# A diffusion trunk step on one core: first weights, conditioning pieces and column sums of the start reordered

## The chip, the core and the metric

The kernel runs on one core of one Trainium2 chip. The metric is the device time of one execution, in microseconds (us). Before the change it is 2101.41 us, the median of three runs (2099.74, 2101.41 and 2103.39).

## What is computed

One inference step of a two-layer trunk over 640 positions (128 of context, 512 latent) of 2048 features. Each layer modulates a normed input, multiplies it by a wide input matrix, mixes, gates, and multiplies by an output matrix:

```
def modulation(cond, w, b):
    m = jax.nn.silu(cond) @ w + b
    return jnp.split(m, 3, axis=-1)

shift, scale, gate = modulation(c, ada_w[l], ada_b[l])
h = rms_norm(x, norm_g[l]) * (1.0 + scale) + shift
y, side = even_mixer(h, w_in_even[e], ...)     # odd layers: odd_mixer
x = x + gate * (y @ w_out[l])
```

There are two condition vectors: one for the context, one for the latent positions. Only the shift and the scale of the first layer concern the change: 2 x 2048 columns of a matrix with 2048 rows, 33.55 MB in float32.

## The kernel before

The features of the input lie on partitions: 16 feature tiles (KT) of 128, each with 640 positions. A weight chunk is 128 output columns by 2048 rows. Every float32 product with weights is made of three passes in a reduced format (`mm_k`, L877): the high part of the weights with the high part of the input, high with low, low with high. For one feature tile k, one chunk and one half of the positions (320 or 322 columns with the two shift columns) these are three matmuls; this text calls each of them a wide matmul. ScalarE (ACT) makes the high part of a weight unit of four feature tiles (512 columns, 262 KB), GpSimd (POOL) its low part (`wpump`, L768). Units of the first chunks go to tiles `suhi`, `sulo`, the others to `whi`, `wlo`.

The start (`start`, L1544) does two things at once. For each of the 16 feature tiles f it brings the modulation matrix's columns of that tile as four **pieces** of 524 KB (`load`, tensor `ada0`) into a ring of NR = 7 buffers, and multiplies each piece by the condition vectors (`tiles`, L1588): four matmuls with 32 stationary columns, one for each 32-column strip of TensorE, so that the result of a tile is four partial sums that lie at partitions 0, 32, 64 and 96 of one bank. ACT copies the bank to SBUF, and two matmuls with a selection matrix `sel` add the four partial sums and bring them to columns (L1604, L1605): this text calls the pair a **column sum**. With it VectorE (DVE) makes scale and shift of the tile, and ACT and DVE the high and low part of the modulated input (`act_mod`, tiles `acth`, `actl`). A piece's buffer is loaded anew when its matmuls have run; the tile of x (`load_x`, 3 buffers) when its modulated input is made.

As soon as inputs are ready, wide matmuls of the first eight chunks run between the pieces: chunks 0 and 1 for every feature tile (`lead`), chunks 2 to 7 in windows of 2, 2, 4 and 4 feature tiles. That makes 2 x 16 x 6 + 6 x 12 x 6 = 624 wide matmuls in the start. What is left of chunks 2 to 7 follows after it, then all the rest of the program, where TensorE takes wide matmuls nearly without a break.

The order of the instructions on every engine is not written by hand. The kernel is built by a planner that keeps a clock for each engine and for the DMA (`Pace`, `pe` at L402, `dma` at L417) and lets tasks yield until their inputs would be ready by these clocks. A matmul's price and the rate of the DMA (330e3 bytes per us, L427) decide which instruction is written next, in the start and after it. The instructions of each engine then run in that order on the chip. All loads of the start are issued by SyncE (SP) in order, and each load also waits for the one eight places ahead of it in the sequence of all DMAs.

Of the kernel before, what the change touches and what calls it, by code (L numbers as in the profile page):

```python
# [14 lines left out]
ALU = mybir.AluOpType  # L15
AX = mybir.AxisListType
# [16 lines left out]
NR = 4  # L33
CW = 2 + HT
RING = 2560
WINDOWS = ((0, 2), (2, 2), (4, 4), (8, 4))
PIECE = 512

near = (*range(8, 12), *range(4))
ORDERS = (*near, *range(12, 16), *range(4, 8)), (*near, *range(4, 8), *range(12, 16))  # L40
LEAD, FIRST = 2, 8
# [172 lines left out]
class Core:  # L214
# [5 lines left out]


SMALL = [
    ("sel", 2),
    ("ada_bT", 96),
    ("norm_gT", 32),
    ("final_gT", 16),
# [8 lines left out]
class Trunk:  # L235
# [9 lines left out]
    def __init__(self, tc, d, es):  # L245
# [14 lines left out]
        nc = self.nc  # L260
# [20 lines left out]
        at, c = 0, {}  # L281
        for name, w in SMALL:
            c[name] = small[:, at : at + w]
            at += w
        self.sel = c["sel"]
        self.adab = c["ada_bT"].rearrange("p (a b) -> p a b", b=48)
        self.ng = c["norm_gT"].rearrange("p (a b) -> p a b", b=KT)
        self.fg = c["final_gT"]
# [113 lines left out]
    def pe(self, cost, out, *ins):  # L402
        pc = self.pace
        o, i = [pc.span(out)], [pc.span(x) for x in ins]
        if pc.late:
            pc.due(o + i)
        at = pc.ready("t", o, i)
        self.now = pc.t["t"] = max(self.now, at) + cost + 0.0025
        pc.note("t", o, i, self.now)

    cap, hold = 2.0, 99.0
    share, soon = 0.0, 99.0
    force = busy = often = False
# [3 lines left out]
    def dma(self, out, in_):  # L417

        pc = self.pace
        o, i = [pc.span(out)], [pc.span(in_)]  # L420
        if pc.late:
            pc.due(o + i)
        n = int(np.prod(out.shape)) * 4

        def emit():
            at = pc.t["q"] = max(pc.t["q"], self.now, pc.ready("q", o, i)) + 0.45
            pc.t["d"] = max(pc.t["d"], at + 1.2) + max(0.09, n / 330e3)  # L427
            pc.note("q", o, i, pc.t["d"] + 1.0)
            self.nc.sync.dma_start(out, in_)  # L429

        if pc.ready("q", o, i) <= self.now + 0.1:
            emit()
        else:
            pc.late.append((emit, o + i, lambda: pc.ready("q", o, i)))
# [333 lines left out]
    def wpump(self, force=False):  # L768

        nc, pc = self.nc, self.pace  # L770
# [22 lines left out]
        if job[0] == "add":  # L793
            o, a, b = job[1]()
# [6 lines left out]
        _, key, raw, n, M = job  # L801
        if not force and self.now < self.wfree_at:
            return False
        if isinstance(raw, int):
            m = self.chunks[key[0]][0].shape[2]
            at = 512 * raw
            raw = self.wraws[:, at : at + n * m]
            plain = True
        else:
            raw, m, plain = raw(), 128, False  # L810
        raw = raw.rearrange("p (a b) -> p a b", b=m)
        lead = plain and (key[0] < LEAD or key[:2] == (LEAD, 0))
        if lead:
            if not self.su_free:
                return False
        else:
            a = self.space(n * M)
# [725 lines left out]

    def start(self):  # L1544
        nc, d, tc, Y = self.nc, self.d, self.tc, self.Y
        self.part_b = self.P([128, FIRST, 2], "part_b")
        with tc.tile_pool(name="su", bufs=1) as su:
            self.open_su(su, 6)
# [4 lines left out]
            sq, rt = self.adas[:, 0:T], self.adas[:, T : T + HT]  # L1553
            rows = Ring([self.adas[:, 960 + 256 * i : 1216 + 256 * i] for i in range(3)])

            NX, NR = 3, 7
            xs = [Y[:, i, :] for i in range(NX)]
            room = Y[:, 3:10, :].rearrange("p a b -> p (a b)")
            more = self.t(su, [128, 3, 1024], "more")
            ring = [room[:, 1024 * i : 1024 * i + 1024] for i in range(4)] + [more[:, i, :] for i in range(3)]  # L1560
            ring = [x.rearrange("p (a b) -> p a b", b=256) for x in ring]

            def load(j):
                if j < 4 * KT:
                    self.dma(ring[j % NR], d["ada0"][j // 4, :, 4 * (j % 4) : 4 * (j % 4) + 4, :])

            def load_x(f):
                if f < KT:
                    self.dma(xs[f % NX], d["xT"][:, f, :])
                    self.flags.add(f"xs{f}")  # L1570
# [1 line left out]
            banks = [[self.pj(), self.pj()], [self.pj(), self.pj()]]  # L1572
            pm, pw = self.sm(), self.sm()
            pws = Ring([self.sm(), self.sm()])
            pcol = Ring([pw[:, 400 + 4 * i : 404 + 4 * i] for i in range(4)])

            def squares():
                for f in range(KT):
# [9 lines left out]
            def tiles():  # L1588
                for f in range(KT):
                    for q in range(4):  # L1590
                        w = ring[(4 * f + q) % NR]
                        yield from self.until(w)
                        for j in range(4):
                            o, c = pm[32 * j : 32 * j + 32, 0:256], cond[:, 4 * q + j, :]
                            self.pe(0.15, o, c, w[:, j, :])
                            nc.tensor.matmul(o, c, w[:, j, :], start=(q == 0), stop=(q == 3))
                        load(4 * f + q + NR)
                        if q % 2:
                            yield
                    r = rows.next()  # L1600
                    nc.scalar.activation(r, pm[:, 0:256], AF.Copy)
                    yield from self.until(r)
                    p = pcol.next()
                    self.mm(p[:, 0:2], r[:, 128:256], self.sel)  # L1604
                    self.mm(p[:, 2:4], r[:, 0:128], self.sel)  # L1605
                    nc.vector.tensor_scalar(
                        self.A[0][:, f, :], p[:, 0:2], self.b1[:, 0, f : f + 1], self.ng[:, 0, f : f + 1], ALU.add, ALU.mult
                    )
                    sh = self.s("sh", 2)
                    nc.vector.tensor_scalar(sh, p[:, 2:4], self.adab[:, 0, f : f + 1], None, ALU.add)  # L1610
                    yield from self.wait(f"sq{f}")
                    self.act_mod(0, f, xs[f % NX], 0, T)
                    nc.scalar.activation(self.ah[:, f, 0:2], sh, AF.Copy)
                    nc.vector.tensor_tensor(self.al[:, f, 0:2], sh, self.ah[:, f, 0:2].bitcast(F32), ALU.subtract)
                    load_x(f + NX)
                    self.flags.add(f"act{f}")
# [25 lines left out]
                    else:  # L1642
                        nc.vector.tensor_tensor(y, y, p, ALU.add)

            for j in range(4):
                load(j)
            load_x(0)
            for j in range(4, NR):
                load(j)
            load_x(1)  # L1650
            load_x(2)
            crow = self.t(su, [32, 128], "crow")
            self.sink = self.P([128, 8], "sink")
            nc.scalar.dma_start(self.sink, d["attn_sink"].partition_broadcast(128))
# [22 lines left out]
            for c in range(LEAD):  # L1677
                self.settle()
                self.chunks[c][4](*banks[c])
                self.drop(*banks[c])  # L1680
        self.actset = "s"

    def ysum(self, c):

# [1173 lines left out]
def _consts():  # L2858
    f = np.float32
    t = np.arange(NLAT)  # L2860
    pos = np.stack([t // 64, t % 64], -1).astype(f)
    inv = (f(10000.0) ** (-np.arange(32, dtype=f) / f(32))).astype(f)
    ang = pos[:, :, None] * inv
    cos, sin = np.cos(ang).astype(f), np.sin(ang).astype(f)
    c4 = np.concatenate([cos[:, 0], cos[:, 0], cos[:, 1], cos[:, 1]], 1).T
    s4 = np.concatenate([-sin[:, 0], sin[:, 0], -sin[:, 1], sin[:, 1]], 1).T
    i = np.arange(128)
    em = np.zeros((128, 512), f)
    em[:, 0:128] = np.where(i[None, :] >= i[:, None], 0, NEG)
    em[:, 384:512] = np.where(i[None, :] <= i[:, None], 0, NEG)  # L2870
    sel = np.zeros((128, 2), f)
    for j in range(4):
        sel[32 * j, 0] = sel[32 * j + 1, 1] = 1
    m1 = np.ones((128, 128), f) + np.eye(128, dtype=f)
    mu = (i[:, None] < i[None, :]).astype(f)
    return {"cos": c4, "sin": s4, "emask": em, "sel": sel, "gla_m1": m1, "gla_mu": mu}


def _na_grid():
# [115 lines left out]
```

## Time and profile before

| | |
|---|---|
| median of three runs | 2101.41 us |
| the profiled execution | 2099.8 us |
| its span, first to last instruction | 2098.0 us |
| granted TensorE clock, mean | 0.996 |
| TensorE (PE) busy | 2050.6 us, 98% |
| DVE, ACT, POOL busy | 72%, 46%, 52% |
| moved by DMA | 412.48 MB, mean 197 GB/s |
| moved by DMA in the first 150 us | 46.59 MB, mean 311 GB/s |

The profile shows one execution. The profiled execution's own time is 1.8 us above its span and 1.6 us below the median. TensorE is busy nearly throughout, but ends of matmuls are modelled, and a stretch that is full is not one at TensorE's peak: the spacing of the starts tells how fast it goes. Fractions of time in the start are read in stretches of the span, counted from its first instruction.

### The profile page before, as it was taken

What the parts mean: (1) busy time and instruction counts of PE and PEld (TensorE: products, weight loads), DVE (VectorE), ACT (ScalarE), POOL (GpSimd) and SP (SyncE); (2) the same over time, 40 slices, a digit from 0 to 9 for tenths busy, and PEclk for the clock granted to TensorE, in tenths of its full rate; (3) what the DMA queues carried; (4) which work ended last, traced back from release to release, by engine and by line L of the source; (5) the groups of instructions that cost most, each with busy time, mean ns of one, the idle gap of its engine ahead of it and who ended that gap; (6) DMA issues with size and microseconds to landing.
All of it is one profiled execution on the core that took longest, in us unless ns stands there. A gap on an engine that the chain in (4) does not pass through costs nothing. (4 is left out here: it accounts for less than half of the span.)

```text
span 2098.0 us, 39027 instructions
## 1 busy us (share of the span) xinstructions
PE 2050.6 (98%) x13990; PEld 1977.5 (94%) x13990; DVE 1500.2 (72%) x3448; ACT 962.7 (46%) x1997; POOL 1080.6 (52%) x817
## 2 busy tenths in 40 slices
PE   7999999999999999999999999999999999999996
PEld 4789999999999999999999999999999999999995
DVE  1337787787888786788777888887666677676565
ACT  3434453443334445444454544445454544454443
POOL 3433343333232223466556676656566567758883
PEclk9999999999999999999999999999999999999998
DMA  9955433335554443677657866756555575568756
GB/s 367 327 200 161 130 127 107 119 126 190 164 177 127 133 146 121 226 241 224 199 145 260 285 210 223 241 196 220 176 172 197 183 245 199 176 214 259 241 191 219
DMA packets 216306, 412.48 MB, mean 197 GB/s; under 512 B 25712, under 2 KB 89008, under 8 KB 216112
## 3 DMA queue, kind: packets, MB, share of 16 engines
q1 hardware_dynamic: 214640, 408.43, 59.0%
q8 instruction: 110, 1.80, 0.3%
q10 hardware_dynamic: 1472, 1.56, 0.2%
q14 instruction: 84, 0.69, 0.1%
HBM read 368.83 MB, written 38.45 MB: 194 GB/s over the span
## 5 line engine op out<-in xcount | busy, mean ns | idle before, releaser
L395 PE MATMUL bank<-acth,whi 128*128 128x320 f32 (+1 forms) x3144 | 963.6, 318 | 8.4 <-DVE arena L209 3.0
L395 PE MATMUL bank<-acth,wlo 128*128 128x320 f32 (+1 forms) x3144 | 938.3, 310 | 2.2 <-POOL wlo L209 2.2
L395 PE MATMUL bank<-actl,whi 128*128 128x320 f32 (+1 forms) x3144 | 937.7, 310 | 0.0
L209 POOL TENSOR_TENSOR wlo<-wraw,whi 128x512 fp32r<-128x512 f32 x364 | 507.1, 1399 | 705.7 <-ACT whi L209 609.1
L395 PEld LDWEIGHTS bank<-acth,whi 128*128 128x128 f32 x3144 | 583.1, 188 | 25.1 <-issue 8.8
L395 PEld LDWEIGHTS bank<-acth,wlo 128*128 128x128 f32 x3144 | 582.7, 188 | 3.0 <-POOL wlo L209 2.8
L395 PEld LDWEIGHTS bank<-actl,whi 128*128 128x128 f32 x3144 | 583.0, 188 | 1.5
L209 POOL TENSOR_TENSOR wlo<-rs,whi 128x512 fp32r<-128x512 f32 x292 | 411.6, 1423 | 192.6 <-ACT whi L209 179.3
L209 ACT ACTIVATE whi<-wraw 128x512 fp32r<-128x512 f32 (+1 forms) x397 | 243.1, 624 | 186.6 <-PE bank L395 105.6
L209 ACT ACTIVATE whi<-rs 128x512 fp32r<-128x512 f32 x329 | 201.3, 625 | 110.1 <-PE bank L395 55.2
L209 DVE CUSTOM_DVE_ANT_0 adas<-adas,bank,partg 128x256 bf16<-128x256 f32 (+1 forms) x320 | 178.1, 557 | 10.4 <-DMA adas<-ada_g 3.2
L395 PE MATMUL bank<-tail,whi 128*128 128x322 f32 (+1 forms) x672 | 152.3, 314 | 0.1
L209 ACT ACTIVATE arena<-arena,bc 128x192 f32<-128x192 f32 (+4 forms) x167 | 83.3, 519 | 143.9 <-DVE bc L209 100.7
L395 PE MATMUL bank<-eh,whi 128*128 128x322 f32 (+1 forms) x444 | 138.8, 313 | 0.0
L395 PE MATMUL bank<-eh,wlo 128*128 128x322 f32 (+1 forms) x444 | 138.1, 311 | 0.2 <-POOL wlo L209 0.2
L395 PE MATMUL bank<-el,whi 128*128 128x322 f32 (+1 forms) x444 | 137.7, 310 | 0.0
L209 DVE TENSOR_TENSOR bank<-bank,sums 128x320 f32<-128x320 f32 (+1 forms) x162 | 76.7, 494 | 61.1 <-PE bank L395 49.8
L209 ACT ACTIVATE Y<-bank 128x128 f32<-128x128 f32 (+5 forms) x134 | 52.2, 411 | 144.4 <-PE bank L395 74.3
L209 DVE TENSOR_TENSOR rs<-rs 128x512 f32<-128x512 f32 x83 | 89.1, 1081 | 40.8 <-POOL wlo L209 39.8
L395 PEld LDWEIGHTS bank<-tail,whi 128*128 128x128 f32 x672 | 112.2, 189 | 1.1 <-DMA tail<-far_dram 0.6
L395 PE MATMUL bank<-tail,wlo 128*128 128x322 f32 (+1 forms) x336 | 104.0, 309 | 0.0
L209 ACT ACTIVATE sums<-bank 128x320 f32<-128x320 f32 (+1 forms) x125 | 54.4, 436 | 107.9 <-PE bank L395 104.8
(216 smaller groups left out, 2835.8 us busy)
## 6 DMA issues: line engine op xcount, KB each, us to landing
tail<-far_dram SPq DMA_DIRECT2D x196, 322.0 KB, 4.4
wraw<-w_even SPq DMA_DIRECT2D x176, 256.0 KB, 3.3
adas<-ada_g SPq DMA_DIRECT2D x128, 256.0 KB, 3.8
adas<-ada SPq DMA_DIRECT2D x128, 256.0 KB, 3.6
rs<-w_odd SPq DMA_DIRECT2D x63, 512.0 KB, 5.7
Y<-ada SPq DMA_DIRECT2D x37, 512.0 KB, 6.2
wraw<-w_odd SPq DMA_DIRECT2D x37, 512.0 KB, 5.7
rs<-w_out SPq DMA_DIRECT2D x30, 512.0 KB, 5.5
```

Of the source, the lines that this page charges most:

```text
L209: return f(*args, **kw)
L395: self.nc.tensor.matmul(out, lhsT, rhs, start=start, stop=stop, **kw)
```

## The change

Six edits, all for the start, of which two reach the planner's clocks everywhere:

- SP's first loads: after the four pieces and the x of feature tile f, EARLY = (1, 3, 0) weight units are issued; the pieces of the second tile stand ahead of its x, and the x of the third tile behind two more pieces.
- The ring of pieces has 10 buffers in place of 7.
- The task that multiplies pieces gives way to others after the fourth piece of a tile only (from the third tile on), unless a piece has not come by the planner's clock. Before it gave way after every second piece.
- The column sum: two transposes (through the identity) and a reduction on DVE over the four partial sums take the place of the two matmuls with `sel`. The scale is then made from SBUF, the shift in place.
- In the start the planner writes a weight split only when its data would be there within 0.3 us (`soon`).
- The planner's prices: a piece's matmul costs 0.102 us (was 0.15), a change between pieces and other matmuls 0.15 us more, no matmul the 0.0025 us that each cost on top, and the DMA moves 400e3 bytes per us.

`FINE` leaves the choice it stands in as it was.

```
+EARLY, SOLO, FINE = (1, 3, 0), 2, 4
...
     def pe(self, cost, out, *ins):
...
         at = pc.ready("t", o, i)
-        self.now = pc.t["t"] = max(self.now, at) + cost + 0.0025
+        if (cost == self.NARROW) != self.narrow:
+            self.narrow = not self.narrow
+            at = max(self.now, at) + 0.15
+        self.now = pc.t["t"] = max(self.now, at) + cost
         pc.note("t", o, i, self.now)
 
+    NARROW, narrow = 0.102, False
...
-            pc.t["d"] = max(pc.t["d"], at + 1.2) + max(0.09, n / 330e3)
+            pc.t["d"] = max(pc.t["d"], at + 1.2) + max(0.09, n / 400e3)
...
     def start(self):
         nc, d, tc, Y = self.nc, self.d, self.tc, self.Y
+        self.soon = 0.3
...
-            NX, NR = 3, 7
+            NX, NR = 3, 10
...
-            more = self.t(su, [128, 3, 1024], "more")
-            ring = [room[:, 1024 * i : 1024 * i + 1024] for i in range(4)] + [more[:, i, :] for i in range(3)]
+            more = self.t(su, [128, 6, 1024], "more")
+            ring = [room[:, 1024 * i : 1024 * i + 1024] for i in range(4)] + [more[:, i, :] for i in range(6)]
...
-            pcol = Ring([pw[:, 400 + 4 * i : 404 + 4 * i] for i in range(4)])
+            pcol = Ring([pw[:, 256 * i : 256 * i + 256] for i in range(2)])
...
-                            self.pe(0.15, o, c, w[:, j, :])
+                            self.pe(self.NARROW, o, c, w[:, j, :])
                             nc.tensor.matmul(o, c, w[:, j, :], start=(q == 0), stop=(q == 3))
                         load(4 * f + q + NR)
-                        if q % 2:
+                        if q == 3 or f < SOLO:
                             yield
...
                     p = pcol.next()
-                    self.mm(p[:, 0:2], r[:, 128:256], self.sel)
-                    self.mm(p[:, 2:4], r[:, 0:128], self.sel)
+                    for i in range(2):
+                        self.tr(p[:, 128 * i : 128 * i + 128], r[:, 128 * i : 128 * i + 128])
+                    sh = self.s("sh", 4).rearrange("p (a b) -> p a b", b=2)
+                    four = p.rearrange("p (a j b) -> p a j b", j=4, b=32)[:, :, :, 0:2]
+                    nc.vector.tensor_reduce(sh, four.rearrange("p a j b -> p a b j"), AX.X, ALU.add)
                     nc.vector.tensor_scalar(
-                        self.A[0][:, f, :], p[:, 0:2], self.b1[:, 0, f : f + 1], self.ng[:, 0, f : f + 1], ALU.add, ALU.mult
+                        self.A[0][:, f, :], sh[:, 1, :], self.b1[:, 0, f : f + 1], self.ng[:, 0, f : f + 1], ALU.add, ALU.mult
                     )
-                    sh = self.s("sh", 2)
-                    nc.vector.tensor_scalar(sh, p[:, 2:4], self.adab[:, 0, f : f + 1], None, ALU.add)
+                    sh = sh[:, 0, :]
+                    nc.vector.tensor_scalar(sh, sh, self.adab[:, 0, f : f + 1], None, ALU.add)
...
-            for j in range(4):
-                load(j)
-            load_x(0)
-            for j in range(4, NR):
-                load(j)
-            load_x(1)
-            load_x(2)
+            for f in range(NX):
+                for j in range(4 * f, min(4 * f + 4, NR)):
+                    load(j)
+                load_x(f)
+                for _ in range(EARLY[f]):
+                    self.wload()
```

The planner makes new orders of this on every engine. Three places follow. SP, the program's first loads (`Y<-ada` and `more<-ada` are pieces, `Y<-xT` is an x, `wraw<-w_even` a weight unit), before:

```order
L429 DMA Y<-ada 128x1024 x4
L429 DMA Y<-xT 128x640
L429 DMA more_116<-ada 128x1024 x3
L429 DMA Y<-xT 128x640 x2
L429 DMA wraw<-w_even 128x512 x4
L429 DMA Y<-ada 128x1024 x4
L429 DMA more_116<-ada 128x1024
L429 DMA Y<-xT 128x640
```

and now:

```order
L432 DMA Y<-ada 128x1024 x4
L432 DMA Y<-xT 128x640
L432 DMA wraw<-w_even 128x512
L432 DMA more_116<-ada 128x1024 x4
L432 DMA Y<-xT 128x640
L432 DMA wraw<-w_even 128x512 x3
L432 DMA more_116<-ada 128x1024 x2
L432 DMA Y<-xT 128x640
```

The first weight unit moved ahead of the second tile's pieces, and that tile's last piece ahead of two loads of x and all four weight units.

ACT, the same stretch, from the first modulated input on (`adas<-bank` is the copy ahead of a column sum, `adas<-Y` a square of x for the norm, `suhi` a weight split), before:

```order
L209 ACTIVATE acth<-Y,A_98 128x512
L209 ACTIVATE acth<-sh_162 128x2
L209 ACTIVATE suhi_181<-wraw 128x512
L209 ACTIVATE suhi_185<-wraw 128x512
L209 ACTIVATE suhi_189<-wraw 128x512
L209 ACTIVATE whi<-wraw 128x512
L209 ACTIVATE adas<-Y 128x640 x2
L209 ACTIVATE adas<-bank_71 128x256
```

and now:

```order
L210 ACTIVATE suhi_162<-wraw 128x512
L210 ACTIVATE acth<-Y,A_98 128x128
L210 ACTIVATE acth<-Y,A_98 128x512
L210 ACTIVATE acth<-sh_168 128x2
L210 ACTIVATE adas<-bank_71 128x256
L210 ACTIVATE adas<-Y 128x640
L210 ACTIVATE suhi_209<-wraw 128x512
```

The second tile's copy moved ahead of three weight splits and of the squares.

PE, from its first matmul on (`cond` are the pieces, `suhi` and `sulo` the weights of chunks 0 and 1), before:

```order
L1596 MATMUL bank_71<-Y,cond_112 32x256 x16
L395 MATMUL bank_72<-small,adas 128x2 x2
L1596 MATMUL bank_71<-more_116,cond_112 32x256 x8
L395 MATMUL bank_67<-acth,suhi_181 128x322
L395 MATMUL bank_68<-acth,suhi_181 128x320
```

and now:

```order
L1600 MATMUL bank_71<-Y,cond_112 32x256 x16
L399 MATMUL bank_72<-ident,adas 128x128 x2
L1600 MATMUL bank_71<-more_116,cond_112 32x256 x8
L394 MATMUL bank_67<-acth,suhi_162 128x322
L394 MATMUL bank_68<-acth,suhi_162 128x320
L394 MATMUL bank_67<-actl,suhi_162 128x322
L394 MATMUL bank_68<-actl,suhi_162 128x320
L394 MATMUL bank_67<-acth,sulo_163 128x322
L394 MATMUL bank_68<-acth,sulo_163 128x320
L1600 MATMUL bank_71<-more_116,cond_112 32x256 x8
L399 MATMUL bank_72<-ident,adas 128x128 x2
```

Transposes stand where the products with `sel` stood, and only chunk 0's six wide matmuls now stand between the second tile's pieces; before, chunk 1's six stood there too. Over the whole start the pieces lie in 49 unbroken groups before and in 36 now, and ahead of the last piece stand 510 wide matmuls before and 384 now.

## Rows read from the trace of the kernel before

**Rows 1.** Stretches: from:to in us, length, busy us by engine (instructions), granted clock, DMA share, GB/s.

```profile
0.00:33.20 33.20, 19.04 (x127) 10.52 (x128) 3.82 (x12) 11.28 (x22) 12.50 (x17) 0.90 0.95 355
50.00:130.00 80.00, 80.00 (x674) 60.87 (x673) 25.98 (x82) 29.12 (x67) 31.44 (x23) 1.00 0.95 328
165.25:2050.00 1884.75, 1870.45 (x12608) 1835.11 (x12607) 1422.42 (x3258) 886.88 (x1833) 1004.82 (x751) 1.00 0.58 188
0.00:50.00 50.00, 35.84 (x272) 23.71 (x273) 7.47 (x22) 18.59 (x44) 17.04 (x20) 0.93 0.97 367
40.00:50.00 10.00, 10.00 (x88) 7.60 (x87) 1.58 (x5) 4.03 (x12) 2.85 (x2) 1.00 1.01 379
120.00:130.00 10.00, 10.00 (x84) 7.95 (x83) 3.32 (x10) 2.33 (x6) 2.60 (x2) 1.00 0.97 364
```

**Rows 2.** Waits of PE in the first 33.2 us: total us, times, longest.

```profile
PE bank L1596 <- DMA Y<-ada: 7.7, 4, 6.4
PE bank L395 <- ACT adas L209: 3.3, 2, 2.8
PE bank L395 <- ACT suhi L209: 3.2, 1, 3.2
```

**Rows 3.** Order of time, PE, 5 to 32 us: start us, length us, instruction, count [idle before].

```profile
18.60 0.90 PE L395 MATMUL bank<-acth,suhi 128*128 128x322 f32 x2 [3.20 <-ACT suhi L209]
...
22.80 0.61 PE L1596 MATMUL bank<-Y,cond 128*32 128x256 f32 x8
26.18 1.01 PE L395 MATMUL bank<-small,adas 128*128 128x2 f32 x4 [2.77 <-ACT adas L209]
```

**Rows 4.** Order of time, ACT, 11 to 32 us.

```profile
25.12 0.74 ACT L209 ACTIVATE adas<-Y 128x640 f32<-128x640 f32 x1 [3.94 <-POOL ssq L209]
25.77 0.37 ACT L209 ACTIVATE adas<-bank 128x256 f32<-128x256 f32 x1
```

**Rows 5.** One stretch of PE: the pieces (L1596) alone, then all other products (L395) alone.

```profile
33.20:165.25 132.05, 31.78 (x416) 1.00 0.79 273
...
33.20:165.25 132.05, 106.57 (x663) 1.00 0.79 273
```

**Rows 6.** Order of time, PE, 152 to 166 us: first and last of 84 wide matmuls.

```profile
152.86 0.31 PE L395 MATMUL bank<-acth,whi 128*128 128x322 f32 x1
...
165.10 0.30 PE L395 MATMUL bank<-acth,wlo 128*128 128x320 f32 x1
```

**Rows 7.** Order of time, PE, 50.8 to 60 us.

```profile
51.43 0.64 PE L1596 MATMUL bank<-more,cond 128*32 128x256 f32 x8
...
52.44 0.39 PE L395 MATMUL bank<-acth,whi 128*96 128x320 f32 x1
...
58.44 0.50 PE L395 MATMUL bank<-small,adas 128*128 128x2 f32 x4
58.87 0.64 PE L1596 MATMUL bank<-Y,cond 128*32 128x256 f32 x8
59.44 0.57 PE L395 MATMUL bank<-acth,suhi 128*128 128x322 f32 x2
```

**Rows 8.** Waits of SP's own queue, 50 to 130 us: total us, times, longest.

```profile
SPq L429 <- PE bank L1596: 42.4, 33, 3.3
```

**Rows 9.** Order of time: SP's issue of the last piece; PE's last group of pieces.

```profile
130.37 0.33 SPq L429 DMA_DIRECT2D Y<-ada  x1
...
147.31 0.61 PE L1596 MATMUL bank<-Y,cond 128*32 128x256 f32 x8
```

**Rows 10.** DMA queues, 12 to 40 us, all packets together.

```profile
DMA packets 4016, 11.28 MB, mean 403 GB/s; under 512 B 448, under 2 KB 579, under 8 KB 4015
```

**Rows 11.** Order of time, PE, 236 to 244 us: transposes.

```profile
237.76 0.71 PE L400 MATMUL bank<-ident,arena 128*128 128x128 f32 x5
238.31 0.27 PE L400 MATMUL bank<-ident,Y 128*128 128x128 f32 x1
```

**Rows 12.** Groups by line and shape, DVE: busy us, mean ns, idle before.

```profile
L209 DVE TENSOR_SCALAR A<-bank,b,small 128x2 f32<-128x2 f32 x16 | 4.4, 276 | 52.4 <-PE bank L395 52.4
```

More of the change, by code (lines that the diff above doesn't have):

```diff
@@ L222 @@
 SMALL = [
-    ("sel", 2),
     ("ada_bT", 96),
@@ L284, in __init__ @@
             at += w
-        self.sel = c["sel"]
         self.adab = c["ada_bT"].rearrange("p (a b) -> p a b", b=48)
@@ L811, in wpump @@
         raw = raw.rearrange("p (a b) -> p a b", b=m)
-        lead = plain and (key[0] < LEAD or key[:2] == (LEAD, 0))
+        lead = plain and (key[0] < LEAD or key[0] == LEAD and key[1] < FINE)
         if lead:
@@ L1680, in start @@
                 self.drop(*banks[c])
-        self.actset = "s"
+        self.actset, self.soon = "s", 99.0
     def ysum(self, c):
@@ L2870, in _consts @@
     em[:, 384:512] = np.where(i[None, :] <= i[:, None], 0, NEG)
-    sel = np.zeros((128, 2), f)
-    for j in range(4):
-        sel[32 * j, 0] = sel[32 * j + 1, 1] = 1
     m1 = np.ones((128, 128), f) + np.eye(128, dtype=f)
     mu = (i[:, None] < i[None, :]).astype(f)
-    return {"cos": c4, "sin": s4, "emask": em, "sel": sel, "gla_m1": m1, "gla_mu": mu}
+    return {"cos": c4, "sin": s4, "emask": em, "gla_m1": m1, "gla_mu": mu}
 def _na_grid():
```

## Prediction

> **What bounds the kernel now.** I read the stretches first [rows 1]. From 165.25 us, where the start's last wide matmul is out (it begins at 165.10 [rows 6]), to 2050 us TensorE is busy for 1870.45 of 1884.75 us: there only 14.3 us are to be had. The start is another case. In its first 33.2 us TensorE is busy for 19.04 us, at a mean granted clock of 0.90, and the DMA is full (share 0.95). From 50 to 130 us TensorE has no idle time, and the DMA moves only 328 GB/s, after 367 in the first 50 us.
>
> Then the waits of the first 33.2 us [rows 2]: TensorE stands still for 7.7 us for pieces, 3.2 us for the first weight split, 3.3 us for ACT's copies ahead of a column sum. In order of time [rows 3] the first wide matmul starts at 18.60 us; the second tile's last piece is multiplied at 22.80, but its column sum starts at 26.18. ACT shows why [rows 4]: the copy starts at 25.77 and stands behind a square at 25.12, which waited 3.94 us for POOL's sum of squares. At 22.80 + 0.6 = 23.4 us the copy could have run: some 2.4 us lost.
>
> From 33.2 us on I account for all of TensorE's time. The counts [rows 5]: 416 records of pieces, eight to a piece, are 52 pieces; of the 663 others, 56 belong to 14 column sums, 607 are wide matmuls or like them. The spacing of wide matmuls: 84 of them start from 152.86 to 165.10 us [rows 6], 12.24/83 = 0.1475 us. A group of two pieces takes 52.44 - 51.43 = 1.01 us, one piece 59.44 - 58.87 = 0.57, so a further piece costs 0.44; a column sum 58.87 - 58.44 = 0.43 [rows 7]. Together 607 x 0.1475 + 52 x 0.44 + 14 x 0.43 = 89.5 + 22.9 + 6.0 = 118.4 of 132.05 us. The other 13.65 us lie at the 45 groups of pieces in this stretch (49, less 4 before it): 0.30 us for each change to narrow matmuls and back. Nothing is left for waits. So from 33.2 us on TensorE sets the pace, and the loads follow: between 50 and 130 us SP waits 42.4 us, 33 times, for TensorE to free a piece's buffer [rows 8]. The last piece is issued at 130.37 us and multiplied only at 147.31 [rows 9].
>
> Before 33.2 us TensorE did 12 pieces, 2 column sums, 21 wide matmuls and 4 groups: 5.3 + 0.9 + 3.1 + 1.2 = 10.5 us of work. The other 22.7 us are lost.
>
> **The change on TensorE.** Column sums: five transposes take 238.31 - 237.76 = 0.55 us [rows 11], so a pair costs 0.22 in place of 0.43: 16 x 0.21 = 3.4 us less. Groups: 49 become 36, 13 x 0.30 = 3.9 us less. "Four pieces in one go" holds for few tiles, since by the planner's clock pieces still come late: 16 of the 36 groups hold a single piece. Together 7.3 us.
>
> **The change in SP's order.** Up to the second tile's last piece SP loaded 8 pieces, 3 x and 4 weight units, 6.23 MB; now 8 pieces, one x and one unit, 4.78 MB. At the 403 GB/s of the full queue [rows 10] that is 3.6 us earlier. The copy, now ahead of the squares on ACT, gains the 2.4 us more: the second column sum starts 6.0 us earlier. The first weight unit has 2.69 MB up to its end and not 4.92, 5.5 us earlier, which takes the whole 3.2 us wait off the first wide matmul [rows 2], but no more, since then its input is what is late. So of the 22.7 us lost, 3.2 to 6.0 go. What is late next is the third tile's last piece: the bytes ahead of it are the same 8.32 MB.
>
> By TensorE's work the start then ends at 165.25 - 7.3 - 3.2 = 154.8 us, at best at 152.0.
>
> **The change for the DMA.** With less work on TensorE the loads may bind. Up to the last piece SP now issues 64 pieces, 15 x, 18 weight units and 2 small ones, 43.3 MB, and ACT some 0.25. In the first 50 us 367 x 50 = 18.35 MB are moved [rows 1]; 25.2 MB are left. At 379 GB/s, the row from 40 to 50 us, nearest to what comes (queue full, TensorE at full pace), that takes 66.5 us, to 116.5. I estimate 1 us for landing. Behind the last piece stand its group, a column sum, 240 wide matmuls and two small sums: 0.74 + 0.22 + 35.4 + 0.6 = 37 us. End: 154.5 us. At 403 GB/s it is 150.5, at 328 it is 164.8.
>
> The two limits agree within a microsecond, so neither hides the other for long; where they meet unevenly I add 1 us (bounds 0 and 4: the x loads waited for DVE in the same queue). The start ends at 155.8 and not at 165.25: 9.45 us less.
>
> **What costs nothing.** The reduction on DVE: nearest is the scale's 276 ns [rows 12], so 16 x 0.28 = 4.5 us, on an engine that is busy for 26 of 80 us [rows 1]. It lengthens the chain from column sum to modulated input, and wide matmuls of other tiles cover that; without them the 4.5 us would all show. Ten buffers cost no time; they let three pieces more be on their way and are why I take 379 and not 328. The moved waits: SP now stands behind a full sequence of 16 loads when it comes to the second x, and behind that x stand three weight units; chunk 1's first wide matmuls wait for the first of them. That is in the bounds 3.2 to 6.0. The rest of the program is planned anew by the new prices; I put it at nothing, with bounds of 4 us less and 14.3 us more, the idle time there once over.
>
> **The sum** is 2099.8 - 9.45 = 2090.4 us for the profiled execution. Its own time stands 1.6 us under the median, so against the median of 2101.41 I forecast **2092 us**.
>
> **Rivals.**
> 1. The rate stays. If 328 GB/s is all that the DMA gives beside a busy TensorE, the start ends at 164.8 + 1, and the time is 2102: no change. For it: the DMA's share is 0.95 at that rate. Against: SP's 42.4 us of waits for buffers, and 379 at a full TensorE. Chance 0.14.
> 2. A ceiling in between. 364 GB/s from 120 to 130 us is the fastest ten microseconds after 50; with it 25.2 MB take 69.2 us, the start ends at 158.2, and the time is 2094.4. Chance 0.10. The Trainium skill's "DMA: Bandwidth & Descriptors" (Specifications) speaks against this change here: it puts a core's share of the memory at about 358 GB/s. By that figure the end would be an estimated 158.4 + 1 us, 2095.6. The trace disagrees, as it holds 403 GB/s for 28 us [rows 10].
> 3. The rest loses more than the start gains. The planner's matmul now takes 0.0025 us less everywhere, some 31 us over 12,400 of them, so all that other engines do after the start is written at other places between the matmuls. TensorE then meets results that are not there. The price is the 14.3 us of idle time between 165.25 and 2050 us once more, 2092 + 14.3 = 2106; it decides against the change from 9.45 us of new waits on, and shows as slower from 13.7. For it: the orders differ to the end on all engines. Against: the price of a wide matmul was 0.1498 in the planner and is 0.1473 now, and 0.1475 was measured. Chance 0.12.
>
> **How the numbers follow.** The forecast has 0.64: within 4 us of 2092, at the lower end with 403 GB/s and all of 6.0 us (2088). The range should hold the time 8 times in 10: down to 2085, for 403 GB/s with a rest that gives back 3 us; up to 2101, the edge of rival 1. A measurement of this kernel can tell about 0.2% from no change, 4.2 us: faster is below 2097.2, slower above 2105.6. Faster: 0.60 of the forecast, 0.08 of rival 2, 0.04 of the others: 0.72. Slower: 0.08 of rival 3 and 0.02 of rival 1: 0.10. Same: 0.18.
>
> **What would show it.** Right: the second column sum starts near 20 us, the last group of pieces near 118 us, the first idle time after the start near 156; the DMA above 370 GB/s from 50 to 115 us; TensorE's idle time from there to the end as before. Column sums at 0.22 us. Wrong: 330 GB/s with SP no longer waiting for TensorE (rival 1), TensorE idle for pieces between 36 and 115 us by more than 4 us in total, or idle time after the start that is 10 us above before (rival 3).

## The result and the profile after

The changed kernel takes **2114.50 us** (median of five runs, 2108.01 to 2116.85). The kernel before, run beside it, has 2101.41 (2099.74 to 2103.39). The ratio is 1.0052, with an interval of 1.0042 to 1.0063: slower by about 11 us by the ratio (the two medians are 13 us apart), where 2092 us and a gain were forecast.

| | before | after |
|---|---|---|
| the profiled execution, its span | 2099.8, 2098.0 us | 2116.24, 2114.4 us |
| granted TensorE clock, mean | 0.996 | 0.991 |
| start's last wide matmul begins | 165.10 us | 164.09 us |
| from there to the program's last wide matmul | 1915.6 us | 1931.7 us |

The start gives 1.0 us of the 9.45 forecast, and the rest takes 16.1 us more. Stretches of the kernel after (columns as in [rows 1]):

```profile
0.00:33.20 33.20, 21.78 (x138) 10.71 (x139) 7.20 (x14) 9.76 (x22) 9.25 (x14) 0.90 0.95 357
50.00:115.00 65.00, 61.17 (x542) 46.02 (x541) 34.43 (x81) 25.67 (x59) 28.02 (x20) 0.97 1.01 391
164.40:2050.00 1885.60, 1861.20 (x12490) 1824.64 (x12491) 1403.44 (x3244) 882.66 (x1823) 986.85 (x743) 1.00 0.57 186
```

The DMA does more than the forecast asked: 391 GB/s in place of 328. But between 50 and 115 us TensorE now stands still for 3.8 us where it had no idle time, and behind the start for 24.4 us (1885.60 - 1861.20) in place of the 14.3 of [rows 1]. In order of time, PE of the kernel after:

```profile
15.80 0.90 PE L394 MATMUL bank<-acth,suhi 128*128 128x322 f32 x2
...
20.14 0.44 PE L399 MATMUL bank<-ident,adas 128*128 128x128 f32 x2 [0.52 <-ACT adas L210]
...
60.27 0.51 PE L394 MATMUL bank<-acth,whi 128*128 128x322 f32 x1 [2.88 <-DVE part_b L210]
...
124.69 0.64 PE L1600 MATMUL bank<-Y,cond 128*32 128x256 f32 x8
...
164.09 0.30 PE L394 MATMUL bank<-acth,wlo 128*128 128x320 f32 x1
165.53 0.39 PE L394 MATMUL bank<-acth,whi 128*128 128x322 f32 x1 [1.14 <-DVE bc L210]
```

The start begins as forecast: first wide matmul at 15.80 (18.60 before), second column sum at 20.14 us (forecast near 20; before 26.18, [rows 3]). Then, at 60.27, a wait that the kernel before does not have: 2.88 us for `part_b`, the addition with which DVE empties a bank of a window. There are three of them up to the end of the start (PE's waits from 33 to 165 us: total us, times, longest):

```profile
PE bank L394 <- DVE part_b L210: 5.8, 3, 2.9
```

What DVE did before the first, and what POOL did beside it (kernel after, order of time):

```profile
55.19 3.16 DVE L210 SCALAR_TENSOR_TENSOR actl<-Y,A,acth 128x128 fp32r<-128x128 f32 x2 [0.53 <-ACT acth L210]
58.27 1.48 DVE L210 TENSOR_TENSOR actl<-sh,acth 128x2 fp32r<-128x2 f32 x1
59.68 0.47 DVE L210 TENSOR_TENSOR Y<-Y,bank 128x320 f32<-128x320 f32 x1
60.08 0.14 DVE L210 TENSOR_TENSOR part_b<-part_b,bank 128x2 f32<-128x2 f32 x1
```

```profile
54.94 1.56 POOL L210 TENSOR_TENSOR ssq<-ssq,adas 128x640 f32<-128x640 f32 x1 [4.24 <-ACT adas L210]
56.47 1.33 POOL L210 TENSOR_TENSOR sulo<-wraw,suhi 128x512 fp32r<-128x512 f32 x1
57.77 1.97 POOL L210 TENSOR_TENSOR ssq<-ssq,adas 128x640 f32<-128x640 f32 x1
59.70 1.27 POOL L210 TENSOR_TENSOR sulo<-wraw,suhi 128x512 fp32r<-128x512 f32 x1
```

An operation on two columns takes 1.48 us and ends at 59.75, when POOL's addition ends (57.77 + 1.97 = 59.74). The Trainium skill's "SBUF — State Buffer" (Who interferes with whom) says that only the pair of SBUF ports which VectorE shares with GpSimd causes contention, that it is an exclusive lock, and that a VectorE instruction with two inputs in SBUF contends for it with a GpSimd instruction that reads SBUF. The rows agree: both inputs of the long operation (`sh`, `acth`) lie in SBUF. The addition behind it, which has one of its inputs in a bank, takes 0.47 us, though POOL works on. DVE's groups from 10 to 165 us after the change (columns as in [rows 12]):

```profile
L210 DVE SCALAR_TENSOR_TENSOR actl<-Y,A,acth 128x512 fp32r<-128x512 f32 x16 | 13.0, 810 | 2.4 <-ACT acth L210 2.4
L210 DVE TENSOR_SCALAR sh<-sh,small 128x2 f32<-128x2 f32 x16 | 11.2, 700 | 0.0
L210 DVE TENSOR_SCALAR A<-sh,b,small 128x2 f32<-128x2 f32 x16 | 9.7, 608 | 0.6
...
L210 DVE TENSOR_REDUCE sh<-bank 128x4 f32<-128x16 f32 x16 | 2.7, 171 | 42.8 <-PE bank L399 42.8
```

The reduction itself is cheap. But the scale, now made from SBUF, takes 608 ns in place of 276 [rows 12].

Behind the start, PE's waits from 168 us on (kernel after; total us, times, longest):

```profile
PE bank L394 <- DVE arena L210: 5.3, 10, 1.2
PE bank L399 <- DVE arena L210: 4.0, 4, 1.9
PE bank L399 <- ACT Y L210: 3.6, 3, 1.5
PE bank L394 <- DVE tail L210: 3.5, 1, 3.5
PE bank L394 <- DVE sums L210: 2.0, 1, 2.0
```

After the longest of them the granted clock falls as well. Stretches of the kernel after, the clock third from the right:

```profile
555.00:559.00 4.00, 4.00 (x18) 3.89 (x18) 3.52 (x14) 1.32 (x5) 0.00 (x0) 0.57 0.12 37
1075.00:1081.00 6.00, 5.71 (x20) 5.36 (x21) 2.47 (x6) 3.06 (x6) 1.89 (x3) 0.50 0.45 164
1173.00:1177.00 4.00, 3.52 (x15) 3.52 (x16) 3.03 (x13) 2.57 (x6) 3.29 (x3) 0.57 0.71 200
1927.00:1931.00 4.00, 4.00 (x19) 4.00 (x18) 2.35 (x4) 1.74 (x5) 3.94 (x4) 0.57 0.95 314
```

A mean of 0.57 says that most of the 4 us ran at 1.2 GHz and not at 2.4, and costs 4 x 0.43 = 1.7 us; the four stretches together cost 8.2. In what follows, half clock stands for a granted clock of 0.5. Before the change the clock did not fall between 33 and 2080 us. So behind the start there are 10.1 us more of idle time up to 2050 us and 8.2 at half clock; some 2 us come back at the end (2050 us to the last wide matmul: PE idle for 1.6 us in place of 3.3).

Where the longest wait comes from, the kernel after in order of time, ACT, DVE and PE:

```profile
1065.72 0.63 ACT L210 ACTIVATE whi<-wraw 128x512 fp32r<-128x512 f32 x1 [5.20 <-DMA wraw<-w_odd]
...
1067.02 3.28 DVE L210 TENSOR_TENSOR actl<-Y,acth 128x640 fp32r<-128x640 f32 x2 [5.39 <-ACT acth L210]
...
1075.29 1.00 PE L394 MATMUL bank<-acth,whi 128*128 128x322 f32 x2 [3.50 <-DVE tail L210]
```

ACT stands for 5.20 us in front of a weight split whose data is not there, DVE for 5.39 us behind ACT, PE for 3.50 us behind DVE. The same split in the kernel before:

```profile
1056.22 0.63 ACT L209 ACTIVATE whi<-wraw 128x512 fp32r<-128x512 f32 x1 [1.99 <-DMA wraw<-w_odd]
...
1070.72 0.78 PE L395 MATMUL bank<-acth,whi 128*128 128x322 f32 x2 [1.92 <-DVE tail L209]
```

From 170 to 2090 us ACT, DVE and POOL wait together 126 us for transfers before, and 173 us after (the sum of all rows of their waits that name a DMA).

This is one execution. e3 below has the same order of instructions on every engine, and one operand of the column sum in another place; its profiled execution takes 1924.7 us for the stretch behind the start, 7.0 less, with two stretches at half clock in place of four. So part of the 16.1 us belongs to this execution; that the changed kernel is slower is shown by its five runs.

### The profile page after: what moved, and what is told of

Same layout as the page of the kernel before. It is cut to its first block, busy times and chain, and to the rows that moved or that the text cites. A ratio compares the mean times of both kernels' runs of the same rounds, so it can differ in the third digit from the quotient of the medians.

```text
span 2114.4 us, 38986 instructions
## 1 busy us (share of the span) xinstructions
PE 2054.3 (97%) x13958; PEld 1981.2 (94%) x13958; DVE 1508.2 (71%) x3464; ACT 966.9 (46%) x2003; POOL 1073.8 (51%) x817
```

## The experiments

Ratios are to the kernel before in the same call. "Start" is when the start's last wide matmul begins in the profiled execution, "rest" the time from there to the last wide matmul of the program, "waits" are those of ACT, DVE and POOL for transfers from 170 to 2090 us. Kernels are numbered as their labels, e1 to e14. "Start", "rest" and "waits" are those of one execution: e3, e4, e5, e6, e10 and e11 have the same start, instruction for instruction, and end it between 157.2 and 165.1 us (the last section says why). A difference of a few us in "start" alone therefore does not show what an edit does.

| | ratio, interval | start | rest | waits |
|---|---|---|---|---|
| before | 1 | 165.1 | 1915.6 | 126 |
| after | 1.0052, 1.0042 to 1.0063 | 164.1 | 1931.7 | 173 |
| e1 old prices behind the start | 0.9988, 0.9977 to 0.9999 | 162.8 | 1917.2 | 123 |
| e2 before, new prices behind the start | 1.0039, 1.0024 to 1.0055 | 165.1 | 1924.6 | 174 |
| e3 reduction into the bank | 1.0032, 1.0019 to 1.0044 | 159.5 | 1924.7 | 178 |
| e4 = e1 and e3 | 0.9984, 0.9970 to 0.9999 | 160.4 | 1917.4 | 109 |
| e5 = e4, DMA price new | 1.0036, 1.0024 to 1.0048 | 160.4 | 1927.7 | 149 |
| e6 = e4, matmul price new | 0.9996, 0.9987 to 1.0005 | 157.2 | 1918.2 | 101 |
| e7 = e4, short additions on POOL | 0.9956, 0.9943 to 0.9968 | 158.0 | 1916.5 | 113 |
| e8 = e4, old prices in the start too | 1.0000, 0.9992 to 1.0009 | 159.4 | 1920.8 | 145 |
| e9 = e4, additions on DVE | 0.9984, 0.9976 to 0.9993 | 158.4 | 1919.0 | 130 |
| e10 = e4, 290e3 | 1.0007, 0.9997 to 1.0017 | 160.2 | 1923.0 | 128 |
| e11 = e4, 480e3 | 1.0097, 1.0080 to 1.0113 | 165.1 | 1941.1 | 187 |
| e12 = e4, column sums by matmul | 0.9971, 0.9962 to 0.9980 | 157.6 | 1920.5 | 107 |
| e13 = e12, additions on DVE | 0.9987, 0.9977 to 0.9996 | 156.7 | 1923.1 | 121 |
| e14 = e12, old prices everywhere | 1.0037, 1.0023 to 1.0050 | 170.8 | 1921.5 | 128 |

### The two theories: prices behind the start, and the place of the reduction

e1, at the end of the start (e2 sets the new prices there in the kernel before):

```
-            pc.t["d"] = max(pc.t["d"], at + 1.2) + max(0.09, n / 400e3)
+            pc.t["d"] = max(pc.t["d"], at + 1.2) + max(0.09, n / self.rate)
...
         self.actset, self.soon = "s", 99.0
+        self.extra, self.rate = 0.0025, 330e3
```

> The change, but from the end of the start on the planner goes by the prices of before again (0.0025 us on each matmul, 330e3 bytes per us). Inside the start everything stands as in the changed kernel. Theory A, the rest of the program was lost through the new prices: the 16 us that the stretch behind the start takes longer (1950 against 1933 us) go, the start still ends near 164.4 us, and the time is about 2100 us (2097 to 2104). Rival B, the rest is lost through something that the start hands on (the order at its seam, the state of the queues): the time stays above 2110 us. Rival C, any replanning of the rest is as good as a throw of dice: somewhere between, 2104 to 2110 us.

Median 2099.36 us: theory A. The rest is back at 1917.2 us, with the start's order that of the changed kernel on every engine.

> The kernel before, whose planner takes the new prices (nothing on a matmul, 400e3 bytes per us) from the end of the start on; the start is that of before. Theory A, the new prices cost the rest some 13 to 17 us: about 2115 us (2111 to 2120), with TensorE's idle time and stretches at half clock behind the start as in the changed kernel. Rival B, the loss comes from the start: about 2101 us, as before. Rival C: between.

Median 2110.67 us, just under theory A's range: with the start of before, the new prices alone cost 0.39% and the rest takes 9.0 us more.

e3 writes the reduction into the bank; the order of every engine stays, behind the start too:

```
-                    sh = self.s("sh", 4).rearrange("p (a b) -> p a b", b=2)
+                    su4 = p[:, 8:12].rearrange("p (a b) -> p a b", b=2)
+                    sh = self.s("sh", 2)
...
-                    nc.vector.tensor_reduce(sh, four.rearrange("p a j b -> p a b j"), AX.X, ALU.add)
+                    nc.vector.tensor_reduce(su4, four.rearrange("p a j b -> p a b j"), AX.X, ALU.add)
```

> The change, but the reduction over the four partial sums is written into the bank and not to SBUF, so that scale and shift are made from the bank as before. The order of all engines stays as it is. Theory: the two small operations of 608 and 700 ns, whose operands all lie in SBUF, are slow because they stand against GpSimd there; from the bank they take about 0.25 us, DVE is some 13 us less busy in the start, TensorE's three waits for the last small sums (5.8 us) go, and the start ends near 158 us in place of 164.4: about 2108 us. Rival: DVE is late because of its large operations on the modulated input and the work it shares with GpSimd: the two small ones get shorter, the waits stay within 2 us, and the time stays at 2112 to 2116 us.

Median 2108.32 us, as the theory said, and the start ends at 159.5. DVE's groups of e3 from 10 to 160 us:

```profile
L210 DVE SCALAR_TENSOR_TENSOR actl<-Y,A,acth 128x512 fp32r<-128x512 f32 x16 | 15.8, 988 | 2.2 <-ACT acth L210 2.1
L210 DVE SCALAR_TENSOR_TENSOR actl<-Y,A,acth 128x128 fp32r<-128x128 f32 x16 | 11.5, 716 | 5.0 <-ACT acth L210 5.0
...
L210 DVE TENSOR_TENSOR actl<-sh,acth 128x2 fp32r<-128x2 f32 x16 | 7.6, 473 | 0.0
L210 DVE TENSOR_SCALAR A<-bank,b,small 128x2 f32<-128x2 f32 x16 | 4.5, 279 | 0.6
L210 DVE TENSOR_SCALAR sh<-bank,small 128x2 f32<-128x2 f32 x16 | 3.4, 210 | 0.0
```

The two small operations are as short as forecast, but the waiting has moved to the next ones: the low parts of the modulated input take 716, 988 and 473 ns (417, 810 and 285 after). Two waits for `part_b` stay, 4.5 us of the 5.8, which is what the rival said of them: most of the waits have another cause than the operand of the small two. Of the 4.6 us by which the start ends earlier, 3.3 are no merit of the edit: the changed kernel's profiled execution had the half clock from 23 to 30 us as well, e3's had not.

> Both of these edits: old prices from the end of the start on, and the reduction into the bank. If both theories hold the two gains add up: the start ends near 158 us, the rest takes 1933 to 1936 us, and the time is about 2094 us, which is what the prediction said of the change itself. If the loss of the rest comes from the start (rival B): about 2108 us. If the waits for DVE stay (rival of the third run): about 2100 us.

Median 2099.61 us, the number for waits that stay. Against e3 the old prices give 0.48%, 10 us. Against e1, from which e4 differs by the reduction in the bank alone, that edit gives nothing that the intervals could tell; so its gain in e3 (1.0032 against 1.0052, intervals that touch) is not shown either.

### Which price

e5 and e6 each put back one of the two old prices in e4's line:

```
-        self.extra, self.rate = 0.0025, 330e3
+        self.extra = 0.0025
```

```
-        self.extra, self.rate = 0.0025, 330e3
+        self.rate = 330e3
```

> The fourth kernel (old prices behind the start, reduction into the bank), but of the two old prices behind the start only the 0.0025 us on each matmul; the DMA stays at 400e3 bytes per us. Theory A1, the matmul's price is what loses the rest: the stretch behind the start's last wide matmul takes about 1935 us as in the fourth kernel (1934), the time is within 3 us of it (about 3 us under before). Rival A2, the DMA's rate is what loses it: about 1943 us as in the third kernel, and the time is about 5 us above before.

> The fourth kernel, but of the two old prices behind the start only the 330e3 bytes per us; a matmul costs nothing on top. Theory A1: the stretch behind the start takes about 1943 us, the time is about 5 us above before. Rival A2: about 1935 us and about 3 us under before. If each price costs a part, both runs lie between, some 4 to 6 us over the fourth kernel in the sum of the two.

e5 is 1.0036, e6 0.9996: it is the DMA's rate (A2). e6 lies 0.12% over e4, which the intervals cannot tell from nothing. I had put the matmul's price first (A1). e10 and e11 turn the rate alone (`self.extra, self.rate = 0.0025, 290e3`, and `480e3`):

> The fourth kernel, whose planner behind the start counts with 290e3 bytes per us in place of 330e3. Theory A2 (too high a rate makes the planner write instructions ahead of data that is not there): nothing is lost, from the start's last wide matmul to the last it takes 1913 to 1919 us (1917 in the fourth kernel, 1925 to 1932 with 400e3). Rival C (each other number throws the dice anew, 400e3 had bad luck): as likely above 1922 us as below.

> The fourth kernel, whose planner behind the start counts with 480e3 bytes per us. Theory A2: at least as much is lost as with 400e3, from the start's last wide matmul to the last it takes 1927 to 1935 us; ScalarE, VectorE and GpSimd together wait more than 150 us for transfers behind the start (109 us in the fourth kernel); the time is 8 to 15 us above the fourth kernel. Rival C: anything from 1915 to 1932 us.

480e3 costs more than forecast: 1.0097 against e4's 0.9984 is 24 us, with TensorE at half clock seven times between 33 us and its last wide matmul, once for twice as long. The longest wait of e11, DVE and PE in order of time:

```profile
1159.02 0.48 DVE L210 CUSTOM_DVE_ANT_0 adas<-adas,bank,partg 128x256 bf16<-128x256 f32 x1 [4.45 <-DMA adas<-ada_g]
...
1161.54 0.63 PE L394 MATMUL bank<-acth,whi 128*128 128x320 f32 x1 [5.41 <-DVE sums L210]
```

At 290e3 theory A2 said that nothing is lost; the rest takes 1923.0 us, above its range, and the time is 0.23% more than e4's, with intervals that just touch. So a rate below 330e3 is not shown to be free, nor to cost: e13 has the same rest at 330e3. Over all runs the rest is 1915.6 to 1923.1 us at 330e3 and 1924.6 to 1931.7 at 400e3; that 400e3 and more cost is shown by the times (the changed kernel against e1, e2 against the kernel before, e3 and e5 against e4, e11), but a part of each kernel's rest stays a matter of its order and of the execution.

### VectorE and GpSimd

e7 keeps e4's order on every engine and makes GpSimd's 15 additions of squares short. It leaves 638 of the 640 columns out of these sums:

```
+                self.pace.record("g", "tensor_tensor", (ssq[:, c], ssq[:, c], sq, ALU.add), {})
+                nc.gpsimd.eng.tensor_tensor(ssq[:, 0:2], ssq[:, 0:2], sq[:, 0:2], ALU.add)
```

> The fourth kernel with the same order on every engine, but in the start GpSimd adds only 2 of the 640 columns of each feature tile's squares (15 additions of some 1.6 us each become short; the sums of squares of the other columns are left out of the computation). Theory: VectorE's operations whose operands all lie in SBUF take turns with GpSimd's, and so the additions are what makes them long. The modulated input's low parts (128x128 716 ns, 128x512 988 ns, 128x2 473 ns in the third kernel) fall to about 400, 760 and 210 ns or less, the two waits of TensorE for the last small sums (4.8 us) go at least by half, and the start's last wide matmul begins near 157 us in place of 160.4: about 3 us faster than the fourth kernel. Rival: VectorE is late because too much stands in its order before these sums: the durations may fall, the waits and the time stay within 1 us of the fourth kernel.

Median 2090.28 us, 0.28% (6 us) under e4, twice what was expected. DVE's groups of e7 from 10 to 160 us:

```profile
L210 DVE SCALAR_TENSOR_TENSOR actl<-Y,A,acth 128x512 fp32r<-128x512 f32 x16 | 12.0, 750 | 2.9 <-ACT acth L210 2.9
L210 DVE SCALAR_TENSOR_TENSOR actl<-Y,A,acth 128x128 fp32r<-128x128 f32 x16 | 7.1, 442 | 6.4 <-ACT acth L210 6.4
...
L210 DVE TENSOR_TENSOR actl<-sh,acth 128x2 fp32r<-128x2 f32 x16 | 4.3, 271 | 0.0
```

Nothing but the length of GpSimd's instructions was changed, and DVE's operations got shorter than e3's by 238, 274 and 202 ns: the two take turns. (The third, on two columns, took 286 ns in e6 too, where GpSimd's additions are long; the other two took 995 and 669 there.) The waits for `part_b`, 3.0 to 4.8 us in the six kernels with e4's start, are 1.9 us, one wait, in e7; what that one stands for is not shown.

e9 gives the additions to DVE (`e = nc.vector if self.soon < 1.0 else nc.gpsimd`):

> The fourth kernel, but in the start VectorE adds the squares and not GpSimd (15 additions). VectorE gets some 15 x 0.7 = 10 us more to do in a stretch in which it is busy for some 86 of 150 us, GpSimd 24 us less. Theory (the two engines take turns on operations that lie wholly in SBUF): with GpSimd's long additions gone the waits of TensorE for the last small sums stay under 2.5 us, the start's last wide matmul begins near 157 to 158 us, and the time is 3 to 6 us under the fourth kernel, some 0.4% under before. Rival: VectorE's own 10 us more put it late by as much: the waits and the time stay within 1.5 us of the fourth kernel.

0.9984, the same as e4: the time is the rival's. In the profiled execution the waits for DVE up to the start's end are 3.7 us (2.0 for `part_b`, 1.0 for `Y`, 0.7 for `adas`) against e4's 4.8, so DVE's own additions took part of what the turns gave; the start ends 2.0 us earlier and the rest takes 1.6 more.

### The parts of the start

e8 leaves the prices out of the start too:

```
-    NARROW, narrow = 0.102, False
+    NARROW, narrow = 0.15, False
...
-            at = max(self.now, at) + 0.15
+            at = max(self.now, at)
...
-    extra, rate = 0.0, 400e3
+    extra, rate = 0.0025, 330e3
```

> The fourth kernel, with the old prices in the start too: everything of the change but its prices, and the reduction in the bank. If the new prices are needed in the start to let the pieces flow (they tell the planner that pieces come at 400e3 bytes per us): the start ends later, near 163 to 165 us, and the time is 3 to 5 us above the fourth kernel. If the ring, the first loads and the transposes alone bring the start's gain: the last wide matmul begins near 160 us as in the fourth kernel and the time is the same as its within 1.5 us.

1.0000, 0.16% over e4, just at the lower edge of what the first theory asked, though the intervals overlap; its start ends at 159.4, as the second says, and the rest takes 3.4 us more. e12 is e4 with the column sums of before:

```
-                    for i in range(2):
-                        self.tr(p[:, 128 * i : 128 * i + 128], r[:, 128 * i : 128 * i + 128])
...
-                    nc.vector.tensor_reduce(su4, four.rearrange("p a j b -> p a b j"), AX.X, ALU.add)
+                    self.mm(p[:, 0:2], r[:, 128:256], self.sel)
+                    self.mm(p[:, 2:4], r[:, 0:128], self.sel)
```

> The fourth kernel with the column sums of before: two matmuls with the selection matrix, no reduction. By the prediction's step the 16 column sums then cost 16 x 0.21 = 3.4 us more on TensorE, and the start's last wide matmul begins near 163.5 us in place of 160.4: 2 to 3.5 us slower than the fourth kernel. Rival: the chain over the reduction on VectorE (0.18 us plus two handovers) eats this up, since VectorE is what the start waits for: the same within 1 us, or faster.

The rival, and the fastest of the kernels that compute everything: **2096.39 us, 0.9971**, 0.3% under the kernel before. That it is faster than e4 the intervals do not show; that it is not 2 us slower they do. The price of the step was right. A column sum on PE, in e3 from its first to the next line, then in e12:

```profile
50.02 0.38 PE L399 MATMUL bank<-ident,adas 128*128 128x128 f32 x2
50.32 1.83 PE L1600 MATMUL bank<-more,cond 128*32 128x256 f32 x24
```

```profile
50.27 0.61 PE L396 MATMUL bank<-small,adas 128*128 128x2 f32 x4
50.81 1.07 PE L1603 MATMUL bank<-more,cond 128*32 128x256 f32 x16
```

0.30 against 0.54 us, 3.8 us for 16. Yet e12's start ends 2.8 us earlier, in executions that both lost 1.7 us to the half clock. It has no wait for `part_b`, though DVE and POOL meet there too, as e12's DVE shows:

```profile
51.71 3.13 DVE L210 SCALAR_TENSOR_TENSOR actl<-Y,A,acth 128x128 fp32r<-128x128 f32 x2 [0.39 <-ACT acth L210]
54.76 1.24 DVE L210 TENSOR_TENSOR actl<-sh,acth 128x2 fp32r<-128x2 f32 x1
```

In e12's order the wide matmuls that PE comes to until 57.8 us find their banks free, in e3's one of them waits 2.56 us at 56.69. So the cheaper sum came with another order, and in that order no wide matmul waited for a collision; why the planner's came out so is not settled, and no run has one order with both sums.

e13 adds e9's edit to e12, e14 adds e8's (the edit of `soon` stays in it too).

> The twelfth kernel (old prices behind the start, column sums by matmul), with the start's squares added by VectorE as in the ninth. Theory: the collisions of VectorE and GpSimd that are left in the twelfth kernel (949 ns against 750 for the modulated input's low part) cost TensorE nothing there, since its order puts other wide matmuls beside them: the time is the same as the twelfth kernel's within 1.5 us. Rival: they still hold up the chain from column sum to input: the last wide matmul of the start begins 1 to 2 us earlier, and the time is 2 us or more under the twelfth kernel.

0.9987: neither. The start ends 0.9 us earlier, the rest takes 2.6 us more.

> The kernel before with the first loads, the ring of ten and the four pieces in one go alone: old prices everywhere, column sums by matmul. Theory: early loads and pieces on their way are what shortens the start; the last wide matmul of the start begins near 159 us (165.1 before, 157.6 in the twelfth kernel), the time is 0.2% under before, within 2.5 us of the twelfth kernel. Rival: without the new prices the planner still takes the pieces for late and spreads them: the start ends at 162 us or later, and the time is within 0.1% of before.

1.0037, slower than either said; the start ends at 170.8 us, late as the rival said (162 us or later). Behind 33.2 us it has 43 groups of pieces against e12's 26 (17 x 0.30 = 5.1 us) and 5.5 us of idle time against 1.5. So with the matmuls by `sel` the start's gain needs the new prices (13 us between e14 and e12, of which 3.4 are half clock), while with the transposes it does not (e8's start 159.4 with no half clock, e4's 160.4 with 1.7 us lost to it).

## Why the prediction was wrong, step by step

- **"I put it at nothing"** (the rest of the program, planned anew) is the step that failed most: 16.1 us, past its bound of 14.3. It was rival 3 that came, at a chance of 0.12, by another price than it named: not the matmul's 0.0025 us (e6) but the DMA's 400e3 bytes per us (e5, e11). ACT, DVE and POOL wait 173 us for transfers where they waited 126, and TensorE behind them. The bound took the idle time once over, 10.1 us of which came; the stretches at half clock behind the waits, 8.2 us, were in no term. How much of either comes is a matter of the execution: e3, in the same order, lost 9.1 us in the rest and not 16.1.
- **"What costs nothing. The reduction on DVE"** failed second. Nearest row and price were right (171 ns measured, 0.28 assumed); the cover was not. I counted DVE's busy time, 26 of 80 us, and not that its operations stand behind POOL's. Waits for DVE cost 5.8 us and the half clock after the first 1.7: 7.5 of the 8.4 us that the start fell short. e7 shows the cause of the long operations, GpSimd's additions of squares, and that they make 1.1 to 2.9 us of the 3.0 to 4.8 us of waits for `part_b` that kernels of e4's order have; the other 1.9 us stay open. The reduction's own operand has a smaller part, which the times do not show (e1, e4).
- **TensorE's work, 7.3 us less**: right in kind. A column sum costs 0.24 us less (0.21 said). From 33.2 us to the start's last wide matmul PE has 130.9 us; without 5.8 of idle time and 1.7 of half clock it is 123.4, with 15 wide matmuls fewer (2.2). 131.9 - 123.4 - 2.2 = 6.3 us.
- **The earlier start, 3.2 to 6.0**: the second column sum came 6.0 us earlier, the first wide matmul 2.8; but only 15 wide matmuls more were done by 33.2 us, 2.2 us.
- **The DMA**: 391 GB/s from 50 to 115 us where 379 was taken; rivals 1 and 2 are out. The Trainium skill's figure of about 358 GB/s as a core's share of the memory ("DMA: Bandwidth & Descriptors", Specifications) was no ceiling for this one core: the trace shows 391 GB/s over 65 us. The last group of pieces came at 124.69 and not near 118. That TensorE's waits and half clock hold up the buffers fits this, but was not tried by itself: in e4 it came at 119.48, in e7, with fewer waits, at 117.07, in e12 at 114.70.
- **The start's end at 155.8** is nearly reached where collisions are fewer: 158.0 in e7, 156.7 in e13. With the old rate behind it, e7 comes to 0.9956 x 2101.41 = 2092.2 us, the number forecast for the change itself, but with work left out: most of both failed steps is taken away. That the two agree to 0.2 us is luck: in e7's profiled execution the start gives 7.1 us and not 9.45.

## What to carry to other kernels

A price in a planner is used wherever the planner is: before changing one for a stretch, ask what it does in the others, or set it for the stretch alone. A DMA rate measured with a full queue was too high for the planner here behind the start, where the DMA's share is 0.57: engines that work in order then stood in front of data that was late, and those that needed their results behind them. And an engine's busy share says nothing of a neighbour that it must take turns with: look at pairs of DVE and POOL instructions that end together before calling an added operation covered.

## What was not expected of the hardware

- VectorE's operations of two columns took 608 and 700 ns from SBUF, 279 and 210 ns from a bank, with GpSimd at work beside both.
- After a wait of TensorE the clock often falls to 1.2 GHz, which cost 1.7 us at a time, now and then twice that. Not always: a wait of 1.92 us brought it at 554 us in the kernel after, one of 1.92 us at 1070.72 in the kernel before did not. So a wait can cost more than its length, by an amount that differs from run to run.
- With the same order and the same edits in the start, six kernels ended it between 157.2 us (e6) and 165.1 (e11). Most of that is the clock. Their stretches up to the start's end (columns as in [rows 1]):

```profile
0.00:157.20 157.20, 142.22 (x1172) 109.83 (x1172) 62.96 (x159) 61.16 (x136) 62.19 (x52) 1.00 0.80 304
0.00:165.10 165.10, 148.40 (x1172) 114.34 (x1172) 66.61 (x159) 60.92 (x136) 63.20 (x52) 0.96 0.77 289
```

  A mean of 0.96 costs 165.1 x 0.04 = 6.6 us. e3, e4, e5 and e10 had one stretch at half clock, 1.7 us. With these taken off, the six end between 157 and 159 us, and by the same reckoning e7 (0.98) at 155 and e12 (0.99) at 156: what was lost to the clock has to come off before starts of single executions are compared.
